# A hybrid mLSTM and attention layer: constant operand rows filled from SyncE's queue instead of GpSimd's

## The chip, the core and the metric

The kernel runs on one core of a Trainium2 chip. The core has five engines with queues of their own: TensorE (PE, matrix products into PSUM), VectorE (DVE), ScalarE (ACT), GpSimd (POOL) and SyncE (SP), which here issues nearly all DMAs. Each engine works its queue in order and waits at an instruction until the semaphores that it names have been reached. The metric is device time of one execution in microseconds. Lower is better.

## The reference

One layer of a decoder on 2048 tokens of width 1024, in float32. The input is normalised and projected once; the projection feeds an mLSTM group (4 heads, in chunks) and an attention group (8 heads, of width 64 plus 32 rotary columns for keys and queries, 64 for values). Both are concatenated, projected out, normalised and added; then follows an MLP with a squared ReLU, normalised and added too.

```python
a = rmsnorm(x, norm_pre_mix)
proj = a @ w_in
h_ml = mlstm_chunkwise(q_ml, k_ml, v_ml, gates...)       # 4 heads
h_mla = causal_block_attention(q, k, v)                  # 8 heads
x = x + rmsnorm(concat([h_ml, h_mla]) @ w_out, norm_post_mix)
m = rmsnorm(x, norm_pre_mlp)
x = x + rmsnorm(square(relu(m @ w_up)) @ w_down, norm_post_mlp)

# inside the attention, for each block of queries:
sc = einsum('bhqd,bkhd->bhqk', qblk, kf) * scale         # causal mask
p = softmax(sc); out = einsum('bhqk,bkhd->bqhd', p, vf)
```

## The kernel before, in words

Products keep float32 accuracy by splitting each operand into a high and a low part and adding three products (`mm3`, lines 253 to 255). The work goes through four stages: the input projection with the mLSTM chunks (to about 520 us), the attention (to about 1000 us), the output projection and the MLP.

All operations are first handed to a planner, `Plan`, with an engine, a cost in ns, what they depend on and a key. `Plan.run` lays them out on a clock of its own: at each step it takes the operation that can start first, and where several of an engine can start together, the one with the lowest key. Calling the operations in this order writes the program. For TensorE, ScalarE, VectorE and GpSimd that order is then pinned; SyncE's DMAs may still be moved among themselves by the layer below. Costs in the plan steer the order only.

The seam between the mLSTM stage and the attention has three switches (`switch1` to `switch3`). Each closes pools of tiles and opens new ones over the same memory. The first writer of a new tile waits until all old tiles under it have been read.

- `switch1` opens QK0, the operands of even heads: a tile of 97 partitions with four parts, Qh, Ql, Kh, Kl (high and low of queries and keys). It lies over tiles of the input stage, among them those that the stores of the rotary queries (line 916) read.
- `switch2` opens V0, the values of heads 0 to 3.
- `switch3` opens V1 (heads 4 to 7), `onecol` and QK1 (odd heads). V1 and `onecol` lie over the normalised input's halves, QK1 over those and over small tiles of the mLSTM chunks, among them hn, which the stores at line 1310 read.

Partition 96 of the operands is constant or computed: Kh holds ones there, Kl and Ql zeros, and Qh minus the row maximum, so that the product of 97 partitions gives scores with the maximum subtracted. The maxima come from products of partitions 0 to 95 alone (line 1594), reduced on VectorE (lines 1601 and 1603), turned by TensorE (line 1627) and put into Qh by ScalarE (line 1630). The constant rows are what `fill` writes:

```python
pool.dma_start(Kh[s][96:97, :], edge[0:1])        # L1496
for z in (Kl, Ql):
    pool.dma_start(z[s][96:97, :], edge[1:2])     # L1498
```

`edge` is an input in DRAM of two rows of 2048, ones and zeros. The plan counts the fills as SyncE's work of 1500 ns; their instructions go into GpSimd's queue at the place that the plan's time gives.

Near the first fill GpSimd also works for the mLSTM chunks: `scale_q` (line 1235, qs from qT and iwbc) and `norm4` (line 1289, the power in the head norm). After `norm4` VectorE multiplies the numerators (line 1295, hn), and the PSUM tile `num` is free for the next chunk's products (lines 1241 and 1244).

In the attention each block of 128 keys and up to 512 queries is a `step`: scores (lines 253 to 255 on QK), two exponentials on ScalarE (lines 1660 and 1664: ph rounded, p or S not), their difference pl on VectorE or GpSimd (line 1668), and products with the values (line 1681 with ph, line 1684 with pl) and with `onecol` (line 1679). `onecol` has 64 columns of zeros and one of ones; its products give the sums of the rows. The first step's pl is one of GpSimd's. Column 128 of each head in V1, the one behind the values, is set to one by a memset (line 1492), and `onecol` by two (lines 1493 and 1494), all on GpSimd.

SyncE's queue in the seam holds, in this order: the stores of the rotary queries, a load of E (line 1207), maskneg (line 1485), the rotary keys of QK0 (line 1540, four), the first block's qkd and qrd (lines 1546 and 1548), iwbc and E of the next chunk (lines 1215 and 1207), further blocks, values (line 1561), the stores of hn (line 1310), and then, after the wait for QK1, the rotary keys of QK1 and the operands of head 1.

Of the kernel before, what the change touches and what calls it, by code (L numbers as in the profile page):

```python
# [10 lines left out]
F32 = mybir.dt.float32  # L11
F32R = mybir.dt.float32r
# [6 lines left out]
P = 128  # L19
SEQ = 2048  # L20
# [23 lines left out]
EKEY = -160.0  # L44
# [8 lines left out]
PFIRST = 16  # L53
HMASK = 1
OB = 1
QLO = 0
TLATE = 0.0
LEAD = 25.0
# [67 lines left out]
def f32(ap):  # L126
    return ap.bitcast(F32)
# [117 lines left out]
def trunk(ctx: ExitStack, tc: tile.TileContext, x, xT, pos, wu, wout, wup, wdn, cols, rows, consts, edge, out, dbg=None):  # L245
# [3 lines left out]
    vec, act, pool, pe = nc.vector, nc.scalar, nc.gpsimd, nc.tensor  # L249
    dma = nc.sync.dma_start  # L250
# [6 lines left out]
    def sb(stack, name, bufs, side="left"):  # L257
        return stack.enter_context(tc.tile_pool(name=name, bufs=bufs, side=side, reuse_waits="tile"))

    def pp(stack, name, bufs, side="left"):  # L260
        return stack.enter_context(tc.tile_pool(name=name, bufs=bufs, side=side, space=PSUM, reuse_waits="tile"))
# [14 lines left out]
    top = ctx.enter_context(tc.tile_pool(name="top", bufs=1))  # L276
    dram = ctx.enter_context(tc.tile_pool(name="dram", bufs=1, space=DRAM))
# [5 lines left out]

    mhalf = top.tile([P, 16], F32, tag="mhalf", name="mhalf")[:, 0:8]
    identr = top.tile([P, P], F32R, tag="identr", name="identr")

    hT = dram.tile([DM, SEQ], F32, tag="hT", name="hT")


    qkd = dram.tile([NH, 64, 4, SEQ], F32, tag="qkd", name="qkd")  # L290
    qrd = dram.tile([2, P, 2, SEQ], F32, tag="qrd", name="qrd")
    krd = dram.tile([32, 2, SEQ], F32, tag="krd", name="krd")
    vd = dram.tile([NT, P, NH, P], F32, tag="vd", name="vd")
    trep = [dram.tile([P, 2, TB], F32, tag=f"trep{b}", name=f"trep{b}") for b in range(NB)]
# [9 lines left out]
    pl = Plan()  # L304
# [19 lines left out]
    def kA(b, t):  # L324

        return KEYA + (b * BLOCK + t) / 1.8
# [62 lines left out]
    def fills2():  # L389
        for p in range(2):  # L390
            pool.memset(cst8[p], 0.0)
        pool.memset(vext[:, :, :, 128:129], 1.0)

    def masks():
        act.copy(identr, ident)

    o_fill2 = pl.op("Pool", 900, fills2, key=kA(0, -40))
    pl.op("Activation", 600, masks, [o_rest], key=kA(1, 0))

    tiles, o_x, x_holders = {}, {}, {}  # L400
# [1030 lines left out]

    V = {}
    pools = {}
    a2 = av = ar2 = pq = pS = po = onecol = maskneg = None
    pm = []
    QK, Qh, Ql, Kh, Kl = ([None, None] for _ in range(5))


    def set_tiles(pool_, s):
        QK[s] = pool_.tile([97, 4, SEQ], F32R, tag=f"QK{s}", name=f"QK{s}")  # L1440
        for i, x in enumerate((Qh, Ql, Kh, Kl)):
            x[s] = QK[s][:, i]
# [16 lines left out]

    def switch3():  # L1460

        nonlocal av, ar2, pS, po, onecol
        s_b.close()
        pools["work0"] = sb(ctx, "work0", 1, "right")
        av = sb(pa, "av", 1, "right")
        ar2 = sb(pa, "ar2", 2, "right")
        pS = pp(pa, "pS", SB_, "right")
        po = pp(pa, "po", 1, "right")

        V[1] = av.tile([P, NT, 4, 129], F32R, tag="V1", name="V1")  # L1470
        onecol = av.tile([P, P], F32R, tag="onecol", name="onecol")[:, 0:65]
        set_tiles(av, 1)

    pl.group = "switch"
    o_s1 = pl.op("Z", 0, switch1, pl.groups["e2"], -KEYA)
    o_s2 = pl.op("Z", 0, switch2, unit_ops + [o_s1], -KEYA)
    o_s3 = pl.op("Z", 0, switch3, pl.groups["in"] + [o_s2], -KEYA)
    pl.group = "prep"
    for name, bufs, when in (
# [6 lines left out]
    o_const = {}  # L1486
    o_const["v0"] = pl.op("Pool", 200, lambda: pool.memset(f32(V[0][:, :, :, 128:129]), 1.0), [o_s2], key=-50)
    for s in (0, "v", 1):

        def fill(s=s):  # L1490
            if s == "v":
                pool.memset(f32(V[1][:, :, :, 128:129]), 1.0)
                pool.memset(f32(onecol[:, 0:64]), 0.0)
                pool.memset(f32(onecol[:, 64:65]), 1.0)
            else:
                pool.dma_start(Kh[s][96:97, :], edge[0:1])  # L1496
                for z in (Kl, Ql):
                    pool.dma_start(z[s][96:97, :], edge[1:2])  # L1498

        o_const[s] = pl.op("Pool" if s == "v" else "SP", 490 if s == "v" else 1500, fill, [o_s3 if s else o_s1], key=EKEY - 30 if s == 0 else -50, kb=0 if s == "v" else 24)  # L1500


    blocks, first, start_of = [], {}, {}
# [1242 lines left out]
def build(arrays, dbg=None):  # L2746
    import concourse.bacc as bacc

    nc = bacc.Bacc("TRN2", target_bir_lowering=False, num_devices=1)
    args = [  # L2750
        nc.dram_tensor(f"in_{n}_dram", v.shape, mybir.dt.from_np(v.dtype), kind="ExternalInput").ap() for n, v in arrays.items()
    ]
    out = nc.dram_tensor("out_0_dram", (SEQ, DM), F32, kind="ExternalOutput").ap()
    with tile.TileContext(nc) as tc:
        trunk(tc, *args, out, dbg=dbg)
    return nc
# [9 lines left out]
```

## Time and profile before

| what | value |
|---|---|
| median of 3 runs | 2408.57 us (2407.36 to 2414.97) |
| profiled execution | 2408.7 us |
| its span, first to last instruction | 2406.9 us |
| mean granted clock of TensorE | 0.995 |
| busy: TensorE | 2360.4 us, 98% |
| busy: VectorE, ScalarE, GpSimd | 72%, 57%, 34% |
| DMAs issued by GpSimd | 26 stores of the output, 6 fills of QK |

The page of a profile gives each engine's busy time; the groups, waits and timelines behind it give single instructions. A line of a timeline reads: start in us, duration in us, engine, line of the kernel, operation, tile written and tiles read, shape, count; in square brackets the idle time of the engine just before it and what ended it. Where a count over 1 stands, several like instructions are merged. TensorE's instructions are pipelined, so their durations overlap. The granted clock is a share of TensorE's full rate.

### The profile page before, as it was taken

Reading aid. Unit: us, or ns where it says so; the run is one execution under the profiler, and the core shown is the slowest. Engines: PE = TensorE matmul, PEld = TensorE weight load, DVE = VectorE, ACT = ScalarE, POOL = GpSimd, SP = SyncE. Lnnn points to the kernel's source line nnn. Section 1 sums busy time; section 2 is a strip of 40 time slices with the busy share of each in tenths; the row PEclk is TensorE's granted clock in tenths of the full one; section 3 lists DMA queues with packets and bytes.
Section 4 is the critical chain, followed back from the end, with each engine's and each line's share of the span. In section 5 each row is a group of like instructions: output and inputs, shape, how many; then the busy total and the mean of one; then the engine's idle time right before and its main releaser. Section 6 shows DMA issues by size and latency. Waiting matters only on the chain. (4 is left out here: it accounts for less than half of the span.)

```text
span 2406.9 us, 34273 instructions
## 1 busy us (share of the span) xinstructions
PE 2360.4 (98%) x11141; PEld 1904.2 (79%) x11141; DVE 1732.2 (72%) x3105; ACT 1361.8 (57%) x2644; POOL 815.3 (34%) x698
## 2 busy tenths in 40 slices
PE   9999999989999999999999999999999999999997
PEld 7777878767777777788788888888888888888885
DVE  6867665658888888647767677766675677776777
ACT  5646454437778877444666556655564344433454
POOL 2725242538788888422000000000000223222346
PEclk9999999999999999999999999999999999999998
DMA  8697979886222321567777797665674445445358
GB/s 288 217 336 248 351 249 335 267 197 152 54 56 54 81 57 32 160 225 249 243 214 221 226 310 221 203 171 167 191 218 139 147 135 181 124 149 164 127 140 164
DMA packets 341308, 449.22 MB, mean 187 GB/s; under 512 B 34908, under 2 KB 227432, under 8 KB 341128
## 3 DMA queue, kind: packets, MB, share of 16 engines
q1 hardware_dynamic: 337192, 440.16, 58.7%
q0 software_dynamic: 3936, 6.87, 2.0%
q8 instruction: 88, 1.44, 0.3%
q14 instruction: 92, 0.75, 0.1%
HBM read 295.97 MB, written 153.05 MB: 187 GB/s over the span
## 5 line engine op out<-in xcount | busy, mean ns | idle before, releaser
L2575 POOL TENSOR_TENSOR y<-vd_0X,y 128x512 f32<-128x512 f32 x7 | 10.6, 1519 | 726.5 <-ACT vd_0X L2572 726.5
L1660 ACT ACTIVATE ph<-S 128x512 fp32r<-128x512 f32 (+1 forms) x320 | 170.3, 532 | 86.7 <-PE S L255 49.9
L1695 POOL TENSOR_TENSOR t<-t,ph 128x512 f32<-128x512 f32 (+1 forms) x192 | 212.9, 1109 | 17.3 <-ACT ph L1660 6.8
L2487 ACT CAST hh<-hr 128x512 fp32r<-128x512 f32 (+1 forms) x208 | 116.2, 567 | 157.0 <-PE d_5X L2538 15.4
L1668 DVE TENSOR_TENSOR pl<-S,ph 128x512 fp32r<-128x512 f32 (+3 forms) x271 | 156.4, 589 | 31.8 <-ACT S L1664 28.9
L253 PE MATMUL mm<-xh,wh 128*128 128x512 f32 x384 | 156.5, 408 | 4.2 <-DVE gate L1185 2.2
L2492 DVE TENSOR_TENSOR hl<-hr,hh 128x512 fp32r<-128x512 f32 (+1 forms) x208 | 133.0, 646 | 30.0 <-ACT hh L2487 23.5
L1601 DVE TENSOR_REDUCE mp<-m 128x1 f32<-128x512 f32 (+2 forms) x208 | 135.7, 666 | 25.2 <-PE m L1594 20.7
L254 PE MATMUL mm<-xl,wh 128*128 128x512 f32 x384 | 150.4, 392 | 0.8 <-DVE xl L424 0.8
L255 PE MATMUL mm<-xh,wl 128*128 128x512 f32 x384 | 150.3, 392 | 0.5 <-DVE wl L499 0.5
L1664 ACT ACTIVATE S<-S 128x512 f32<-128x512 f32 (+3 forms) x271 | 140.2, 517 | 0.4
L253 PE MATMUL S<-QK 97*128 97x512 f32 (+1 forms) x320 | 120.5, 377 | 2.1 <-DVE pl L1668 1.9
L1681 PE MATMUL o<-ph,V 128*128 128x512 f32 (+1 forms) x320 | 119.0, 378 | 1.8 <-DVE ot L1754 1.5
L1684 PE MATMUL o<-pl,V 128*65 128x512 f32 (+1 forms) x320 | 116.0, 363 | 3.4 <-POOL pl L1668 3.4
L1594 PE MATMUL m<-QK 96*128 96x512 f32 (+3 forms) x320 | 115.6, 388 | 1.8 <-DVE mp L1601 1.1
L254 PE MATMUL S<-QK 97*128 97x512 f32 (+1 forms) x320 | 116.9, 365 | 0.0
L255 PE MATMUL S<-QK 97*128 97x512 f32 (+1 forms) x320 | 116.7, 365 | 0.0
L253 PE MATMUL op<-wo,hh 128*128 128x512 f32 x256 | 100.9, 394 | 1.4 <-DVE osm L1985 1.0
L255 PE MATMUL op<-wo,hl 128*128 128x512 f32 x256 | 99.8, 390 | 0.0
L254 PE MATMUL op<-wo,hh 128*128 128x512 f32 x256 | 99.7, 389 | 0.0
L2326 ACT ACTIVATE t<-t 128x512 f32<-128x512 f32 x96 | 60.7, 632 | 65.0 <-DVE t L2321 64.6
L253 PEld LDWEIGHTS mm<-xh,wh 128*128 128x128 f32 x384 | 72.1, 188 | 22.8 <-DVE gate L1185 3.3
(6451 smaller groups left out, 7483.4 us busy)
## 6 DMA issues: line engine op xcount, KB each, us to landing
hr<-hd SPq DMA_DIRECT2D x100, 448.0 KB
wr<-in_wu_dram SPq DMA_DIRECT2D x71, 512.0 KB
hd<-t SPq DMA_DIRECT2D x128, 256.0 KB
hd<-ts SPq DMA_DIRECT2D x96, 256.0 KB
wl<-wparts SPq DMA_DIRECT2D x45, 512.0 KB
QK<-qkd SPq DMA_DIRECT2D x32, 512.0 KB
xt<-in_x_dram SPq DMA_DIRECT2D x28, 512.0 KB
xf<-xd SPq DMA_DIRECT2D x40, 256.0 KB
```

The costliest lines, as they stand in the source:

```text
L253: pe.matmul(o, ah, bh, start=start, stop=False)
L254: pe.matmul(o, ah, bl, start=False, stop=False)
L255: pe.matmul(o, al, bh, start=False, stop=stop)
L1601: vec.tensor_reduce(mp["t"][:, j, kb : kb + 1], ps[:, :n], axis=AX.X, op=ALU.max)
L1660: act.activation(t["h"][:, :w], t["S"][:, :w], AF.Exp)
L1664: act.activation(t["p"][:, :w], t["S"][:, :w], AF.Exp)
L1668: (pool if by_pool else vec).tensor_tensor(t["l"][:, :w], t["p"][:, :w], f32(t["h"][:, :w]), ALU.subtract)
L1681: pe.matmul(o0, v[:, 0:128], t["h"][:, :w], start=start, stop=stop)
L1684: pe.matmul(o1, v[:, 64:129], t["l"][:, :w], start=start, stop=stop)
L1695: pool.tensor_tensor(to, to, hv, ALU.add)
L2487: act.copy(t["h", m][:, :w], t["r", m][:, :w])
L2492: vec.tensor_tensor(t["l", m][:, :w], t["r", m][:, :w], f32(t["h", m][:, :w]), ALU.subtract)
```

## The change

The two rows of `edge` are copied once, near the start, by one DMA from DRAM to a scratch in DRAM (`edged`). The six fills of partition 96 read from that scratch and are issued on SyncE's queue by the same `dma` that issues the other loads, where the plan already counted them; they now depend on the copy too. `onecol` gets a tile of its own in the pool that lives through the whole program, and its two memsets move to the fills at the start (`fills2`). The memset of V1's column becomes an operation of 250 ns (was 490 with `onecol`'s) with key 40 (was -50). Keys and costs of the fills stay.

```diff
+VONE = 40.0
...
+    onecol = top.tile([P, 65], F32R, tag="onecol", name="onecol")
...
+    edged = dram.tile([2, SEQ], F32, tag="edged", name="edged")
...
         pool.memset(vext[:, :, :, 128:129], 1.0)
+        pool.memset(f32(onecol[:, 0:64]), 0.0)
+        pool.memset(f32(onecol[:, 64:65]), 1.0)
...
     o_fill2 = pl.op("Pool", 900, fills2, key=kA(0, -40))
+    o_edge = pl.op("SP", 500, lambda: dma(edged, edge), key=kA(0, 30))
...
         V[1] = av.tile([P, NT, 4, 129], F32R, tag="V1", name="V1")
-        onecol = av.tile([P, P], F32R, tag="onecol", name="onecol")[:, 0:65]
         set_tiles(av, 1)
...
         def fill(s=s):
             if s == "v":
                 pool.memset(f32(V[1][:, :, :, 128:129]), 1.0)
-                pool.memset(f32(onecol[:, 0:64]), 0.0)
-                pool.memset(f32(onecol[:, 64:65]), 1.0)
             else:
-                pool.dma_start(Kh[s][96:97, :], edge[0:1])
+                dma(f32(Kh[s][96:97, :]), edged[0:1])
                 for z in (Kl, Ql):
-                    pool.dma_start(z[s][96:97, :], edge[1:2])
-
-        o_const[s] = pl.op("Pool" if s == "v" else "SP", 490 if s == "v" else 1500, fill, [o_s3 if s else o_s1], key=EKEY - 30 if s == 0 else -50, kb=0 if s == "v" else 24)
+                    dma(f32(z[s][96:97, :]), edged[1:2])
+
+        if s in (0, 1):
+            o_const[s] = pl.op("SP", 1500, fill, [o_edge, o_s3 if s else o_s1], key=-50 if s else EKEY - 30, kb=24)
+        else:
+            o_const[s] = pl.op("Pool", 250, fill, [o_s3], key=VONE)
```

More of the change, by code (lines that the diff above doesn't have):

```diff
@@ L1433, in trunk @@
     pools = {}
-    a2 = av = ar2 = pq = pS = po = onecol = maskneg = None
+    a2 = av = ar2 = pq = pS = po = maskneg = None
     pm = []
@@ L1460, in switch3 @@
     def switch3():
-        nonlocal av, ar2, pS, po, onecol
+        nonlocal av, ar2, pS, po
         s_b.close()
```

## The prediction

> **What bounds the kernel now.** I read the page first, then the waits of TensorE and of GpSimd between 470 and 550 us, then the timelines of five engines in that stretch, because the change touches nothing that runs elsewhere but a few instructions at the start.
>
> ```profile
> span 2406.9 us, 34273 instructions
> PE 2360.4 (98%) x11141; PEld 1904.2 (79%) x11141; DVE 1732.2 (72%) x3105; ACT 1361.8 (57%) x2644; POOL 815.3 (34%) x698
> ```
>
> TensorE is the bound, and has 46.5 us without work in the whole span. A change off TensorE can gain only what it gives back of these, and what slow clock they bring with them. The waits of the stretch, first TensorE's two longest, then GpSimd's at the line that this change takes off it (us in total, times, longest):
>
> ```profile
> PE num L1241 <- DVE hn L1295: 3.0, 1, 3.0
> PE o L1684 <- POOL pl L1668: 3.0, 1, 3.0
> ...
> POOL QK L1496 <- DVE mp L1601: 10.7, 1, 10.7
> ...
> POOL QK L1496 <- DMA maskneg<-in_consts_dram: 6.3, 1, 6.3
> ```
>
> TensorE's two holes add to 6.0 us, and each lies right behind one of GpSimd's waits. The releasers named for GpSimd are inferred; what the instruction waits for is its destination: QK0 is laid over tiles of the input stage, QK1 over those of the mLSTM stage, and each must have been read out.
>
> **First hole.** Timelines of GpSimd, VectorE, TensorE and SyncE (start us, us, what; idle before and its releaser in brackets):
>
> ```profile
> 480.44 0.75 POOL L1496 DMA_DIRECT2D QK<-in_edge_dram  x1 [6.32 <-DMA maskneg<-in_consts_dram]
> 481.19 1.00 POOL L1498 DMA_DIRECT2D QK<-in_edge_dram  x2
> 482.18 0.75 POOL L1235 TENSOR_TENSOR qs<-qT,iwbc 128x256 f32<-128x256 f32 x1
> 482.87 1.04 POOL L1289 TENSOR_TENSOR sm<-sm,mhalf 128x4 f32<-128x4 f32 x1
> ...
> 477.39 0.16 DVE L1285 SCALAR_TENSOR_TENSOR sm<-sm 128x4 f32<-128x4 f32 x1 [0.58 <-ACT jk L1279]
> 483.94 0.76 DVE L1295 TENSOR_TENSOR hn<-num,sm 128x256 f32<-128x256 f32 x2 [3.75 <-POOL sm L1289]
> ...
> 481.06 0.66 PE L1265 MATMUL kv<-vext,kw 128*64 128x129 f32 x8
> 484.75 1.61 PE L1241 MATMUL num<-vext,E 128*128 128x129 f32 x8 [3.04 <-DVE hn L1295]
> 490.21 0.22 PE L1594 MATMUL m<-QK 96*128 96x128 f32 x1
> ...
> 479.84 2.57 SPq L1540 DMA_DIRECT2D QK<-krd  x4
> 482.45 0.60 SPq L1546 DMA_DIRECT2D QK<-qkd  x1
> 483.09 1.24 SPq L1548 DMA_DIRECT2D QK<-qrd  x2
> ```
>
> GpSimd stands at the three fills of QK0 from 474.1 to 480.44, issues them until 482.18, does qs and only then the power sm, whose input VectorE had finished at 477.55. VectorE's hn waits for sm, and TensorE's num waits for hn, because hn empties the PSUM bank that num writes. So the fills sit on TensorE's path.
>
> **Second hole.** GpSimd, ScalarE, TensorE and SyncE:
>
> ```profile
> 521.25 0.59 POOL L1496 DMA_DIRECT2D QK<-in_edge_dram  x1 [10.71 <-DVE mp L1601]
> 522.79 0.23 POOL L1492 MEMSET V<- 128x64 f32 x1
> 523.02 1.27 POOL L1668 TENSOR_TENSOR pl<-p,ph 128x512 fp32r<-128x512 f32 x1
> ...
> 518.03 0.59 ACT L1664 ACTIVATE p<-S 128x512 f32<-128x512 f32 x1
> ...
> 510.33 0.39 PE L255 MATMUL mm<-xh,wl 128*128 128x512 f32 x1
> 520.98 0.40 PE L1681 MATMUL o<-ph,V 128*128 128x512 f32 x1
> 524.35 0.69 PE L1684 MATMUL o<-pl,V 128*65 128x512 f32 x1 [2.97 <-POOL pl L1668]
> ...
> 520.81 2.47 SPq L1540 DMA_DIRECT2D QK<-krd  x4
> 523.95 0.54 SPq L1546 DMA_DIRECT2D QK<-qkd  x1
> ```
>
> The same again: the fills of QK1 hold GpSimd to 522.79. The low part pl of the first attention block, whose input p ScalarE had ready at 518.62, starts at 523.02, and TensorE waits 2.97 us for it.
>
> **The clock behind the holes.** Busy time of each engine in the two stretches that follow; the last columns are granted clock, DMA share and GB/s:
>
> ```profile
> 484.75:490.21 5.46, 5.46 (x25) 4.51 (x26) 0.93 (x4) 1.80 (x10) 0.73 (x1) 0.69 0.85 212
> 524.35:530.09 5.74, 5.74 (x22) 4.49 (x23) 2.19 (x4) 1.17 (x2) 0.00 (x0) 0.54 1.12 201
> ```
>
> With no idle in either, work at full clock would have taken 0.69 x 5.46 and 0.54 x 5.74, so the slow clock costs 1.69 and 2.64 us. A hole of 3 us thus costs 4.73 and 5.61 us; together 10.3.
>
> **The change, part by part.** *Second hole, GpSimd.* Taken away: three DMA issues and their wait. What stays ahead of pl is the memset of V1 (0.23 us). V1 is laid over the halves of the normalised input, which the last gate's product reads until 510.72, so it should be done near 511; no row shows its wait alone. Then pl starts at 518.62 plus a step, and ends near 520.0, 1.4 us before TensorE wants it at 521.38. Behind it stand only products whose inputs VectorE makes without regard to this hole. Gain 5.61. If instead the memset too had to wait to 521.25, pl would start at 521.48, 1.54 us earlier than now: the lower bound 1.54.
>
> *Second hole, SyncE.* The three fills now stand before krd and everything for head 1. The wait is krd's own, so nothing waits longer for it; the issues are new. Two rows bound one issue: a single row as here, and a strided piece of QK (ns min/median/max).
>
> ```profile
> L1765 SPq DMA_DIRECT2D sumd<-ou x32: 235/246/440, 540.5 to 986.1; - x32
> L1548 SPq DMA_DIRECT2D QK<-qrd x8: 589/597/610, 483.1 to 495.5; - x8
> ```
>
> With the 0.04 us that lies between issues, three take 0.9 us by the first, 1.9 by the second. I take 0.9, since a fill is one row. Head 1's first block then goes out at about 525 instead of 523.95. Its first reader comes after the 40 maxima products of head 0, counted here (the bracket behind the first busy time):
>
> ```profile
> 490.00:545.00 55.00, 14.50 (x37) 7.29 (x37) 0.94 0.85 194
> 545.00:548.00 3.00, 0.73 (x3) 0.38 (x2) 1.00 0.05 11
> ```
>
> So it reads after 548: this costs nothing as long as the delay stays under some 18 us.
>
> *First hole, GpSimd.* qs needs an iwbc already there and the previous chunk's products, ahead of kv on TensorE; so sm runs from about 477.6 to 478.6, and hn is done by 479.5. num then follows kv at 481.72, and TensorE reaches its first product on QK0 at 490.21 - 4.73 = 485.48.
>
> *First hole, SyncE.* Here the fills stand in front of the very loads that this product needs: krd, qkd and two of qrd. When do these land? Three rows:
>
> ```profile
> L1594 PEldq EVENT_SEMAPHORE  x2: 51/51/51, 488.3 to 488.5; - x2
> ...
> DMA to landing us min/median/max: 2.8/2.8/3.2
> ...
> 488.97 0.73 POOL L1235 TENSOR_TENSOR qs<-qT,iwbc 128x256 f32<-128x256 f32 x1 [5.06 <-DMA iwbc<-wd]
> ...
> 484.44 1.27 SPq L1215 DMA_DIRECT2D iwbc<-wd  x2
> ```
>
> TensorE's queue, which runs ahead, found the loads landed at 488.3 to 488.5 without waiting; that is the upper end. The last qrd is issued at 483.71; with the shortest landing above (the fills') it is there at 486.5, the lower end. The next load on the queue, iwbc, took from 485.07 to 488.9, that is 3.8 us; by it qrd lands at 487.5, which I take as the nearest row. Plus 0.9 for the fills: 488.4. So TensorE would wait from 485.48 to 488.4, **2.9 us, a new hole as long as the old one**, now for a DMA. If the clock follows as it did here, 1.69 more are lost: 488.4 + 1.69 = 490.1 against 490.21. Gain 0.1. Bounds: 486.5 + 0.9 and no slow clock give 487.4, a gain of 2.8; 488.5 + 1.9 with the dearer 2.64 gives 493.0, a loss of 2.8. What else is queued behind the fills on SyncE (iwbc and E of the next chunk) has slack: it serves chunk products that TensorE's order has behind four of the maxima products.
>
> *Start.* One more DMA on SyncE, and two memsets on GpSimd that leave the seam. SyncE has a gap where the planner's key puts the copy:
>
> ```profile
> 13.68 0.43 SPq L384 DMA_DIRECT2D bg<-in_rows_dram  x1
> 14.82 3.90 SPq L489 DMA_DIRECT2D wr<-in_wu_dram  x3
> ```
>
> Idle 0.71 us covers one issue of 0.25 to 0.6, so nothing; without that cover 0.6. Planned costs on the compute engines change only at one memset that comes ahead of the first attention block either way, so I expect the same order of work.
>
> *Sum.* 5.61 + 0.1 + 0 = 5.7 us. The profiled execution took 2408.7 us (span 2406.9 and 1.8 around it), 0.13 over the median of 2408.57, so 2403.0.
>
> A rule of the Trainium skill speaks to the new hole. "TensorE: Matmul & The Clock Gate", section "Part 1: The HAM clock gate (the "warmup" mystery)", has the clock halved only after a whole idle window of about 3.4 us. By it a hole of 2.9 us costs no clock, and the sum would be 7.4; this trace, with half clock behind holes of 3.04 and 2.97 us, does not bear the threshold out.
>
> **Rivals.** *A, the new hole is cheap.* The loads land earlier, or the shorter hole leaves the clock alone. Without slow clock, 488.4 against 490.21 gains 1.8, and with the early landing 2.8: 5.61 + 1.8 to 2.8, so 2400.3 to 2401.3. For it: the lower end of the landing is as well founded as the middle, and with it the hole shrinks to 1.9. Against: 2.9 is almost 3.0, and both holes of 3.0 slowed the clock. It is the rule's result as well.
>
> *B, part of the second hole stays.* The memset of V1 or another step holds pl. With 1.54 to 3 us there and nothing in the first, 2405.7 to 2407.2. For it: no row shows that memset alone. Against: the bytes of V1 have no reader after 510.72.
>
> *C, not faster: SyncE becomes the bound.* The fills' issues on SyncE may be long: with a length F each, the first product on QK0 comes at 487.5 + 3F + 1.69, against 490.21 now. With the 5.61 of the second hole taken off, the kernel is slower once 3F exceeds 6.6, F above 2.2 us. At 3.35 us, which one load of QK took soon after, the loss is 3.4: 2412.1.
>
> ```profile
> 532.09 3.35 SPq L1546 DMA_DIRECT2D QK<-qkd  x1
> ```
>
> For it: a fill is a new form on this queue. Against: the rows of this queue in the seam, 2.57 for four, 0.60, 1.24 for two, give 0.6 an issue. Past 0.3% it goes only from F = 4.7.
>
> *D, no change at all.* The fills' wait moves nothing since another wait ends at the same time: 2408.7. Against: sm and pl had their inputs 5.3 and 4.4 us before they started.
>
> **How the numbers follow.** Forecast 0.47, A 0.27, B 0.15, C 0.07, D 0.04. The likeliest gives 2403.0. The range reaches down to A's lower end, 2400.0, and up through B, 2407.5; C and D and the tails are left out. About 0.3%, 7.2 us, is what a measurement of this kernel tells from no change, so faster needs 2401.4 or less: A and a part of the forecast's own spread, 0.32. Slower needs 2415.9: the far side of C and what I have not thought of, 0.05. The rest, 0.63.
>
> **What would show it.** GpSimd's line L1289 near 478 and num with no wait; a wait of L1594 for a DMA into QK of about 2.9 us, with clock near 0.7 behind it; pl at 518.6 on today's scale and L1684 without a wait; the fills on SyncE at 0.25 us each. Wrong is the forecast if L1594 doesn't wait, if L1684 still waits for GpSimd, or if TensorE's order has changed.

## The result, and the profile after

The changed kernel takes 2430.89 us (median of 6 runs, 2430.23 to 2434.79) against 2410.09 for the kernel before on the same chip: a ratio of 1.0087, with a 95% interval of 1.0074 to 1.0100. It is 21 us slower, where 5.7 us less were forecast. The page of its profile:

```profile
span 2429.6 us, 34250 instructions
...
PE 2383.8 (98%) x11141; PEld 1906.4 (78%) x11141; DVE 1724.9 (71%) x3105; ACT 1361.1 (56%) x2644; POOL 811.0 (33%) x692
```

TensorE's idle time is 2429.6 - 2383.8 = 45.8 us, against 46.5 before. So the 22.7 us that the span has grown are not holes: TensorE is *busy* 23.4 us longer, with the same 11141 products in the same order. Where? Stretches of the two traces (busy time of TensorE with its products in brackets, of its weight loads, of VectorE, ScalarE and GpSimd; granted clock, DMA share, GB/s). Before:

```profile
570.00:1000.00 430.00, 424.56 (x2160) 325.74 (x2160) 359.59 (x771) 331.25 (x691) 345.66 (x295) 1.00 0.30 72
...
1500.00:1600.00 100.00, 100.00 (x443) 82.77 (x442) 71.78 (x115) 64.27 (x113) 0.00 (x0) 1.00 0.67 195
1900.00:2000.00 100.00, 99.95 (x442) 82.43 (x441) 71.49 (x112) 41.53 (x76) 31.10 (x22) 1.00 0.39 126
```

After:

```profile
570.00:1000.00 430.00, 424.33 (x2166) 326.07 (x2166) 360.74 (x772) 332.77 (x693) 348.39 (x297) 1.00 0.31 73
...
1500.00:1600.00 100.00, 100.00 (x435) 81.31 (x434) 72.01 (x115) 65.74 (x116) 0.00 (x0) 1.00 0.66 190
1900.00:2000.00 100.00, 100.00 (x432) 80.60 (x431) 69.62 (x109) 37.52 (x69) 27.89 (x20) 1.00 0.40 127
```

In the attention (570 to 1000) the rate is the old one. A thousand us behind the seam TensorE gets through 432 to 435 products in 100 us instead of 442 or 443, without a gap, at full granted clock in both. That stretch holds nothing that the change names. Before, a 128x512 product starts 226.9 ns after the one before it, nearly without spread; after, 230.8 in the mean.

Since the order is the same, one can also ask how much later the n-th product starts than in the trace of before. The differences, worked out from the traces (us; each column is one product, named by its start in the kernel before; 490 is the last product ahead of the first one on QK0; the rows e1 to e10 are the experiments below, and in e9 and e10 some products near 550 and 500 us have changed places):

```
             470     490     506     547     567     968    1769    2370
after       1.39   -3.26    3.66   -1.87    3.43    3.40   10.62   24.30
e1          2.14   -2.51    3.86   -1.67    2.74    2.91   11.76   24.43
e2          0.90    0.66    0.66    0.99    0.94    0.97   10.03   24.15
e4          1.74   -0.18    0.11   -5.43    0.80    0.77    9.01   21.72
e5          1.03   -3.62   -0.48   -6.03   -1.77   -1.85    7.61   21.82
e6          2.56    2.29    2.29    1.41    1.40    1.28    3.08    3.69
e7          1.06   -3.59    1.63   -3.89    1.04    0.91    2.08    2.20
e9          1.50   -1.73   -1.60   -7.12   -7.46   -7.43   -7.02   -7.00
e10         1.00   -3.66   -2.04   -7.92   -8.26   -8.10   -6.56   -5.89
```

Read the row "after" from left to right: the old first hole goes (-4.7), a new one takes its place (+6.9), the second hole goes (-5.5), a third appears (+5.3), nothing in the attention, and then 20.9 us trickle in to 2370; 1.6 us come back at the very end. What differs by 470 is the spread of the input stage; the kernels e2 and e6, which leave the seam alone, have 0.9 and 2.6 there.

**The seam.** TensorE's longest waits from 470 to 620 us, after:

```profile
PE m L1600 <- DMA iwbc<-wd: 4.1, 1, 4.1
PE S L254 <- DVE pl L1674: 3.2, 1, 3.2
```

Both of the old waits (num, and the product on pl) are gone; two new ones have come. The first, in the timelines of GpSimd, SyncE and TensorE:

```profile
476.77 0.72 POOL L1241 TENSOR_TENSOR qs<-qT,iwbc 128x256 f32<-128x256 f32 x1 [1.30 <-PE num L1250]
479.02 1.02 POOL L1295 TENSOR_TENSOR sm<-sm,mhalf 128x4 f32<-128x4 f32 x1 [1.52 <-DVE sm L1291]
...
481.01 0.24 SPq L1499 DMA_DIRECT2D QK<-edged  x1
481.30 0.53 SPq L1501 DMA_DIRECT2D QK<-edged  x2
481.88 2.53 SPq L1546 DMA_DIRECT2D QK<-krd  x4
484.45 0.59 SPq L1552 DMA_DIRECT2D QK<-qkd  x1
485.09 1.24 SPq L1554 DMA_DIRECT2D QK<-qrd  x2
...
491.18 0.44 PE L1600 MATMUL m<-QK 96*128 96x128 f32 x1 [4.07 <-DMA iwbc<-wd]
```

GpSimd's steps come early, as forecast. The fills delay krd by 0.9 us, and TensorE, early too, stands 4.07 us before its first product on QK0. (The releaser's name is inferred: the product reads QK and no iwbc, and its weight load waits for DMA QK<-qkd.) Behind that:

```profile
491.18:497.00 5.82, 5.82 (x19) 4.31 (x21) 1.47 (x6) 1.97 (x5) 2.19 (x3) 0.50 1.07 217
```

Half clock for 5.82 us costs 2.91, so this hole costs 6.98. Second hole (GpSimd, then TensorE):

```profile
514.44 0.21 POOL L1497 MEMSET V<- 128x64 f32 x1 [0.26 <-PE mm L256]
522.33 1.28 POOL L1674 TENSOR_TENSOR pl<-p,ph 128x512 fp32r<-128x512 f32 x1 [7.68 <-ACT p L1670]
...
524.63 0.40 PE L1687 MATMUL o<-ph,V 128*128 128x512 f32 x1
524.87 0.40 PE L1690 MATMUL o<-pl,V 128*65 128x512 f32 x1
```

pl waits for ScalarE alone and the product on it for nothing: the second hole has gone as worked out. The third hole (GpSimd, SyncE, VectorE, ScalarE, TensorE):

```profile
532.58 1.28 POOL L1767 TENSOR_TENSOR ot<-ot,ou 64x512 f32<-64x512 f32 x1
...
542.48 0.49 SPq L1770 DMA_DIRECT2D hT<-ot  x1
544.60 0.25 SPq L1771 DMA_DIRECT2D sumd<-ou  x1
...
548.69 0.69 DVE L1764 COPY ou<-o 65x512 f32<-65x512 f32 x1 [3.47 <-DMA sumd<-ou]
549.30 0.68 DVE L1674 TENSOR_TENSOR pl<-S,ph 128x512 fp32r<-128x512 f32 x1
...
549.96 0.58 ACT L1757 COPY ot<-o 64x512 f32<-64x512 f32 x1 [3.86 <-DMA hT<-ot]
...
550.03 0.50 PE L254 MATMUL S<-QK 97*128 97x512 f32 x1 [3.17 <-DVE pl L1674]
```

The first block of the attention puts its result into ot and ou, of which there is one buffer each. They are ready at 532.58 + 1.28 = 533.86, but the stores that empty them are issued at 542.48 and 544.60: 8.6 us behind, since SyncE's queue has the loads for head 1 in front of them. The second block's copy into ou waits on VectorE for that store, pl stands behind the copy, and TensorE's S waits for pl. The clock is 0.71 in the 5.97 us from 550.03 to 556.00, another 1.7 us. Before:

```profile
534.47 1.28 POOL L1761 TENSOR_TENSOR ot<-ot,ou 64x512 f32<-64x512 f32 x1
...
538.96 0.49 SPq L1764 DMA_DIRECT2D hT<-ot  x1
540.48 0.26 SPq L1765 DMA_DIRECT2D sumd<-ou  x1
...
547.02 0.68 DVE L1758 COPY ou<-o 65x512 f32<-65x512 f32 x1
```

There the same copy came 6.5 us behind the store and waited for nothing. So the old second hole had been covering SyncE's lateness; e4 and e9 below test this.

### The profile page after: what moved, and what is told of

It is laid out like the page before. It is cut to its first block, busy times and chain, and to the rows that moved or that the text cites. A ratio compares the mean times of both kernels' runs of the same rounds, so it can differ in the third digit from the quotient of the medians.

```text
span 2429.6 us, 34250 instructions
## 1 busy us (share of the span) xinstructions
PE 2383.8 (98%) x11141; PEld 1906.4 (78%) x11141; DVE 1724.9 (71%) x3105; ACT 1361.1 (56%) x2644; POOL 811.0 (33%) x692
## 4 chain that ended last, share of the span: by engine, by line
PE 55%; DVE 1%; DMA 0%; issue 0%; ACT 0%; POOL 0%; DVEq 0%; POOLq 0%; ACTq 0%
PE op L254 1%; PE op L256 1%; PE op L255 1%; PE d_4X L2543 1%; PE d_3X L2543 1%; PE d_2X L2543 1%; PE d_0X L2543 1%; PE d_1X L2543 1%; PE d_0X L2545 1%; PE d_1X L2545 1%; PE d_3X L2545 1%; PE d_4X L2545 1%; PE d_0X L2544 1%; PE d_2X L2545 1%; PE d_2X L2544 1%; PE d_1X L2544 1%
```

## The experiments

Two theories for the 20.9 us that come in behind 968. **T**: onecol's new tile of 260 B stands ahead of all pools on the left-hand side of the memory and moves them by 288 B (as the tiles' addresses show), while the right-hand pools stay, or move by 512 B; the products slow down with the new distance between their operands. **R**: the loss comes of the fills on SyncE. On the chip of each series the kernel before took 2410.1 us.

**Undoing the move, first try (e1).** T as first thought: the distance counts modulo 64. 384 B is the largest tile there that leaves room for the later pools.

```diff
-    onecol = top.tile([P, 65], F32R, tag="onecol", name="onecol")
+    onecol = top.tile([P, 96], F32R, tag="onecol", name="onecol")[:, 0:65]
```

> The changed kernel, with onecol's tile given 384 B a partition instead of 260, so that the pools behind it move by 384 B and not by 288. Nothing else differs. Theory T (place in memory: TensorE's products lengthen where the moving and the stationary operand start 32 B apart, counted modulo 64): the later stages run as before, and only what the seam lost stays, 2411 to 2413 us; the product rate from 1900 to 2000 us is 442 again instead of 432. Rival R (the loss comes of the fills on SyncE and of what they do to the DMAs, wherever onecol lies): 2430 us, 432 products in that stretch.

Measured: 2431.40 us, ratio 1.0087 (1.0073 to 1.0101). Its stretch:

```profile
1900.00:2000.00 100.00, 100.00 (x433) 80.85 (x432) 69.55 (x110) 38.04 (x69) 27.92 (x20) 1.00 0.41 127
```

So T modulo 64 has fallen; 2430 us is what R gives, and another form of T may give it too.

**The move alone, in the kernel before (e2).**

```diff
     identr = top.tile([P, P], F32R, tag="identr", name="identr")
+    spare = top.tile([P, 65], F32R, tag="spare", name="spare")
```

> The kernel before with an unused tile of 260 B a partition ahead of the left-hand pools, which moves them by 288 B. The seam is untouched: fills on GpSimd, onecol in its old place. Theory T: the loss of the changed kernel behind the seam appears alone, 20 us, 2429 to 2431 us. Rival R: 2410 us, as before.

Measured: 2430.63 us, ratio 1.0088 (1.0075 to 1.0102).

```profile
1500.00:1600.00 100.00, 100.00 (x435) 81.28 (x434) 72.44 (x116) 65.53 (x116) 0.00 (x0) 1.00 0.66 192
1900.00:2000.00 100.00, 100.00 (x431) 80.54 (x430) 69.60 (x109) 37.74 (x68) 27.89 (x20) 1.00 0.41 127
```

An unused tile, with the seam untouched, brings the whole loss, with the same rates. R has fallen. What remains open is what it is about the place.

**Both sides at 32 modulo 64 (e5).**

```diff
-    edger = sb(ctx, "edger", 1, "right").tile([P, 24], F32, tag="edge", name="edger")
+    edger = sb(ctx, "edger", 1, "right").tile([P, 32], F32, tag="edge", name="edger")
```

> The changed kernel with the edge rows' tile 32 B longer, so that the right-hand pools move by 32 B as well: now both sides lie at 32 modulo 64 in the late stages. Theory T in its form 'the distance between the two operands counts': 2411 to 2413 us. In its form 'each operand must start at a multiple of 64 B': slower still than the changed kernel, above 2431 us. Rival R: 2430 us.

Measured: 2430.91 us, ratio 1.0089 (1.0075 to 1.0103); 433 products from 1900 to 2000. Neither form of T came true: not cured, not worse. The time is R's 2430 us, but e2 has ruled R out. So I sorted all 128x512 products behind 1000 us, in each trace, by the distance of the moving operand's start from the stationary one's, modulo 256 B, taken from the tiles' addresses, and took the mean time from start to start (ns; xa, work0 and dr lie on the right-hand side, work, o1 and w2 on the left):

```
moving, stationary    before       after        e1           e5
xa, work0           0: 226.8     0: 227.5     0: 227.7     0: 227.7
xa, work            0: 226.8   224: 233.0   128: 232.8   192: 233.3
work0, o1           0: 227.1   224: 233.4   128: 233.0   192: 233.3
o1, o1              0: 227.0     0: 227.3     0: 227.2     0: 227.3
w2, dr              0: 226.7    32: 232.3   128: 231.6    64: 232.1
work0, dr           0: 226.7     0: 231.5     0: 232.0     0: 232.3
```

Distances of a multiple of 256 keep 227 ns; 32, 64, 128, 192 and 224 all give 232 to 233. The last row seems to break the rule; its products alternate with those on w2, and with the two neighbours on either side counted in, it keeps: in the changed kernel, products whose own distance and all whose neighbours' are multiples of 256 take 227.8 ns (1930 of them), mixed surroundings 231.6 (2465), none a multiple 233.3 (1541). Against 226.9 that is 1930 x 0.9 + 2465 x 4.7 + 1541 x 6.4 = 23 us, about the 20.9 found. **T2**: the distance counts modulo 256.

**Two tests of T2**, each with a move of 256 B. In the kernel before (e6):

```diff
+    spare = top.tile([P, 64], F32R, tag="spare", name="spare")
```

> The kernel before with an unused tile of 256 B a partition ahead of the left-hand pools. Theory T2 (after e1 and e5: two operands of a product whose starts differ by a multiple of 256 B take 227 ns for 128x512, any other distance 232 to 233 ns): the pools move, the distances modulo 256 don't, 2410 us as before. Rival (any move of the left-hand pools costs, by the place of a bank or the like): 2430 us, as with 288 B.

Measured: 2409.87 us, ratio 0.9999 (0.9990 to 1.0008).

```profile
1500.00:1600.00 100.00, 100.00 (x442) 82.46 (x441) 74.34 (x119) 66.03 (x117) 0.00 (x0) 1.00 0.68 197
1900.00:2000.00 100.00, 99.95 (x441) 82.47 (x440) 72.18 (x114) 40.33 (x73) 28.42 (x21) 1.00 0.42 133
```

And in the changed kernel, with its seam as it is (e7):

```diff
-    mhalf = top.tile([P, 16], F32, tag="mhalf", name="mhalf")[:, 0:8]
+    mhalf = top.tile([P, 8], F32, tag="mhalf", name="mhalf")
+    onecol = top.tile([P, 72], F32R, tag="onecol", name="onecol")[:, 0:65]
     identr = top.tile([P, P], F32R, tag="identr", name="identr")
-    onecol = top.tile([P, 65], F32R, tag="onecol", name="onecol")
```

> The changed kernel, with onecol in a tile of 288 B and the neighbouring tile of mhalf 32 B shorter, so that the pools behind move by 256 B. Seam as in the changed kernel. Theory T2: 2411 to 2413 us: all that is left is the seam, where the changed kernel's trace was 2.0 us behind between 470 and 610 us, and about 1 us of the input stage. Rival (the move itself costs): 2430 us.

Measured: 2410.85 us, ratio 1.0003 (0.9995 to 1.0012).

```profile
1900.00:2000.00 100.00, 99.95 (x441) 82.43 (x441) 71.19 (x112) 41.05 (x74) 29.92 (x22) 1.00 0.42 130
```

In both, every product behind 1000 us is at a distance of a multiple of 256, and a product takes 226.9 ns in the mean. T2 holds in both: moving the pools by 256 B costs nothing, by 288 or 384 some 20 us. And e7 says what the rest of the change is worth: nothing. From 470 to 567 us it gains nothing (1.06 and 1.04 in the table), although both old holes have gone: the two new ones, 3.4 us at the first product on QK0 and 3.5 us near 550, take it back.

**Head 0's rows by GpSimd's queue again** (e4), on the 384 B version:

```diff
-                dma(f32(Kh[s][96:97, :]), edged[0:1])
+                put, rows, at = (dma, edged, f32) if s else (pool.dma_start, edge, lambda x: x)
+                put(at(Kh[s][96:97, :]), rows[0:1])
...
```

> As e1_onecol_384, and the three rows of head 0's operands come by GpSimd's queue again, as before the change; head 1's come by SyncE. Theory T: the later stages as before; the first hole as before (num waits 3.0 us for GpSimd, no wait of 4 us for a DMA at L1600), the second hole gone, worth 5.5 us in the changed kernel's trace, of which the 5.3 us lost again at 550 us stay away if SyncE is no later than before: 2404 us, and 2409 us if that third hole comes all the same. Rival R: 2430 us less the few us of the first fills.

Measured: 2428.51 us, ratio 1.0077 (1.0065 to 1.0090). So 2404 and 2409 were missed, because the 384 B are in it again; the time is also what R gave, which e2 has ruled out. For the seam, the table tells more: with head 0's fills off SyncE the stretch from 470 to 506 gains 1.6 us (1.74 and 0.11) where e1 loses 1.7. A part of that is the clock: num waits 2.7 us here and the clock stays at 1.00 behind it, where in the kernel before it cost 1.69 us. The second hole gives 5.5, and the third takes 6.2 back. Its rows (GpSimd, SyncE, VectorE):

```profile
529.01 1.29 POOL L1768 TENSOR_TENSOR ot<-ot,ou 64x512 f32<-64x512 f32 x1
...
538.42 0.54 SPq L1771 DMA_DIRECT2D hT<-ot  x1
539.30 0.25 SPq L1772 DMA_DIRECT2D sumd<-ou  x1
...
545.38 0.69 DVE L1765 COPY ou<-o 65x512 f32<-65x512 f32 x1 [3.71 <-DMA sumd<-ou]
```

The store stands 8.1 us in the queue here too, although SyncE is earlier than in the changed kernel. So the third hole doesn't come of the first fills. (Head 1's fills are still on SyncE in e4; no run takes these off it alone.)

**The stores ahead of head 1's later loads** (e9), by a dependency for the planner, with the 256 B move and head 0's rows on GpSimd:

```diff
-        ..., *war, *(o_last if b and not h else [])], key, kb=640)
+        ..., *war, *(o_last if b and not h else []), *([o_out[0, 0][0]] if b and h == 1 else [])], key, kb=640)
```

> As e7_change_net256; head 0's constant rows by GpSimd's queue again, head 1's by SyncE; and the loads of head 1's later blocks (b of 1 to 3) stand behind the first store of the attention (hT, sumd) on SyncE's queue, by a dependency for the planner. Theory S (what the second hole gave was lost again at 550 us since the copies of ou and ot waited for stores that stood 8 us in SyncE's queue behind those loads): no wait of S for pl near 550 us, 5.5 us won at the second hole stay, 2405 us. Rival (the wait at 550 us comes of the DMA queues being full, whatever the order): it stays, 2410 us.

Measured: 2404.60 us, ratio 0.9975 (0.9966 to 0.9984).

```profile
527.32 1.29 POOL L1768 TENSOR_TENSOR ot<-ot,ou 64x512 f32<-64x512 f32 x1
...
529.09 1.45 SPq L1771 DMA_DIRECT2D hT<-ot  x1
530.64 0.39 SPq L1772 DMA_DIRECT2D sumd<-ou  x1
...
540.07 0.68 DVE L1765 COPY ou<-o 65x512 f32<-65x512 f32 x1
```

The store goes out 0.5 us after its data are there, the copy doesn't wait, and the 5.5 us of the second hole stay (-1.60 at 506, -7.12 at 547, -7.46 at 567). Theory S holds; full DMA queues, its rival, were not the cause. The planner moves some products of TensorE near 550 us in this kernel, so a part of the gain may be the new order's. Another 3.1 us (1.50 at 470, -1.60 at 506) come from the first hole, which the expectation had left as it was: num waits 1.4 us and the clock stays at 1.00 behind it. No run isolates why, and that the time meets 2405 so closely is in part luck.

**All rows on SyncE, stores early, first maxima products later (e10).**

```diff
-EKEY = -160.0
+EKEY = -156.0
```

(with the 256 B move and the dependency above)

> As e7_change_net256, all constant rows by SyncE; stores ahead of head 1's later loads as in e9; and the planner's key of the first maxima products 4 units later (EKEY -156 in place of -160), so that TensorE has other products to do while QK0's loads land. Theory S: no wait of 4 us at the first product on QK0, none at 550 us: first hole (3.0 us and the slow clock behind it) and second hole both won, 2400 to 2403 us. Rival (the hole only moves to the next wait): 2405 to 2410 us.

Measured: 2401.85 us, ratio 0.9967 (0.9955 to 0.9978). TensorE's waits from 470 to 620:

```profile
PE m L1600 <- DVE mp L1607: 1.1, 2, 0.7
PE m L1600 <- DMA iwbc<-wd: 0.9, 1, 0.9
```

Between num and the first product on QK0 stand six groups of three mv products, where e7 has three, and a chunk's S and kt besides; the wait there is 0.9 us, with no slow clock behind it (1.00 from 490.68 to 497.00). It beats both kernels, by 8 us the one before.

## Why the prediction was wrong

2403.0 us were forecast, 2400.0 to 2407.5 as the range; 2430.9 came. Step by step:

- **Second hole, GpSimd: right.** 5.61 forecast, 5.5 measured (3.66 to -1.87 in the table). The memset of V1 waits for the last gate's product and is out of the way 7.7 us before pl.
- **Second hole, "Behind it stand only products whose inputs VectorE makes without regard to this hole": wrong.** VectorE's copy of ou stands in front of pl and waits for a store on SyncE. TensorE came 5.5 us earlier, SyncE's store 3.5 us later (542.48 against 538.96), and 5.3 us went back at 550 us. What SyncE's lateness would hold up was asked for the reads of QK1 only ("this costs nothing as long as the delay stays under some 18 us"), which was true and beside the point: the stores behind those loads were what ran late.
- **First hole, GpSimd: right.** Arrival at the first product on QK0 485.48 forecast; 491.18 - 4.07 - 1.39 (the input stage's offset) = 485.7 measured.
- **First hole, SyncE: mechanism right, size off.** The fills take 0.24 and 0.53 us as taken. From the start of its issue, as the forecast counted, the last load took 491.18 - 485.74 = 5.4 us and not 3.8, so the hole is 4.07 us and not 2.9, with 2.91 us of slow clock and not 1.69. Instead of a gain of 0.1 a loss of 2.3, inside the bound of 2.8 that was named.
- **Start, and the place of onecol: the step that failed.** It priced two memsets and a DMA, on the premise that "the change touches nothing that runs elsewhere but a few instructions at the start". The place of the tile itself was a term of the sum put at nothing without a reason, and it costs 20 us: 2430.9 with the pools moved by 288 B, 2410.9 with the same seam and a move of 256 B (e7). The forecast was 27.9 us short; these 20.0, the 5.3 of the third hole and the 2.4 of the first make 27.7. The kernel gave a hint: several of its small tiles are longer than what is used of them (the old onecol took 128 columns and used 65; mhalf 16 and 8), and that padding was read past.
- **"I expect the same order of work": right**, and with the rates of each engine at hand it shut out everything but the length of single products.
- **Rivals.** Of the signs named, all on the seam came as the forecast had them but for the size of the new hole (4.07 us for 2.9, a clock of 0.50 for 0.7); the time was decided a thousand us later. C has the right side and its price of 2412.1 is near e7's 2410.85, but by luck: not the fills' own length, but a store behind loads. No rival held the cause of the 20 us.

The rule of the clock that the prediction weighed can now be seen on one hole of three lengths: e5, e7 and the changed kernel wait 2.92, 3.44 and 4.07 us before the same product. The stretch behind it in e5:

```profile
489.67:497.00 7.33, 7.33 (x47) 5.83 (x48) 4.20 (x13) 2.53 (x6) 2.20 (x3) 1.00 0.99 228
```

And in e7:

```profile
490.22:497.00 6.78, 6.78 (x32) 5.12 (x33) 3.17 (x11) 1.97 (x5) 2.20 (x3) 0.75 1.02 227
```

So no slow clock after 2.92 us, 0.25 x 6.78 = 1.7 us of it after 3.44, 2.91 after 4.07. But in the kernel before, holes of 2.97 and 3.04 us had cost 2.64 and 1.69. And e2 shows a clock of 0.70 from 485.40 to 491.00, 1.7 us lost, behind a hole of 2.78 us, shorter than e5's. A threshold in the hole's length alone doesn't fit these numbers. "TensorE: Matmul & The Clock Gate" of the Trainium skill, section "Part 1: The HAM clock gate (the "warmup" mystery)", says that the window of about 3.4 us runs freely. These rows agree in that the length alone doesn't decide; that it is where a hole lies that does, no run here tests. The whole idle window that the prediction named from that section of the Trainium skill isn't borne out: holes of 2.78 to 3.04 us had no room for one of 3.4.

## What to carry to other kernels

A tile's size is a part of the change even where its contents are not: before pricing a moved or added tile, list which pools' addresses it shifts, and keep the moving and stationary operands of the long product loops at a distance of a multiple of 256 B (pad, or take the bytes from a neighbour). A stall that is removed sets one engine ahead of the others: go through every queue that was not sped up, the stores in it too, and ask which single-buffered tile its lateness will hold. When busy time grows and idle time doesn't, compare the time from start to start of one kind of instruction before looking for waits.

## What the runs showed of the hardware

- A 128x512 fp32r product on a TensorE that never waits took 226.9 ns from start to start with operands at a distance of a multiple of 256 B, and 232 to 233 ns (2.2 to 2.8% more) at 32, 64, 128, 192 and 224 modulo 256; other distances did not occur behind 1000 us. Products at a multiple of 256 that stand between such products slow down too (231.5 to 232.3 ns). The start of one operand alone doesn't matter: 256 B of move are free (e6), and pairs on one side keep 227 ns under moves of 288 and 384 B. "TensorE: Matmul & The Clock Gate" of the Trainium skill, section "Step-by-step: what each phase is for", has TensorE read its two operands through ports of their own, so that loading the next weights takes nothing from the running product. These runs differ from that: something in the two reads does depend on how they lie to each other. Whether it is the product's own weights or the next ones, loaded meanwhile, the traces don't separate, since almost always both have the same distance.
- The attention didn't slow down under the moves: 2160 to 2166 products from 570 to 1000 us in the kernel before and after. Rows of V there are 516 B apart, so most distances are no multiples of 256 in either kernel; whether it would gain from rows of another length was not tried.
